# Retention/attention backbone, first projection stage: weights split at fixed points, a third PSUM bank for the second chunk, a shorter and earlier decay polynomial, transposes for the modulation pairs

## The chip, the cores and the metric

One Trainium2 chip, of which the kernel uses one core. The metric is the time of one execution on the device in microseconds (us). Kernels are compared by the median of several runs. The engines named below are PE (matrix multiply; PEld is its weight load), DVE (vector), ACT (scalar), POOL (GpSimd) and SP, whose queue issues nearly all DMAs.

## The reference, cut to what matters

The whole computation is two layers over 256 latent and 256 context tokens of width 2048: a bidirectional multi-scale retention layer, then a windowed attention layer. The change lies in the first stage, which makes the modulated input of layer 0 and the first head's queries and keys from it:

```python
mod = silu(c) @ ada_w[0] + ada_b[0]               # for c and for c_ctx
shift, scale, gate = split(mod, 3)
h = rms_norm(x, norm_gain[0]) * (1 + scale) + shift   # 512 tokens, width 2048
p = h @ ret_w_in                                    # q, k, v and gate of 8 heads
lg = log_sigmoid(decay_logit)                       # per head and direction
decay(i, j) = exp(lg * (i - j))                     # weights of the retention
```

All matrix products are wanted in nearly full float32. The kernel gets this by splitting each float32 operand into a high and a low part that TensorE can multiply, and by adding three products (high by high, low by high, high by low).

## The kernel before

Tokens lie on the free axis (512 columns, latents first), features on the partitions in 16 blocks `kb` of 128. Weights come in pieces of 128 x 2 x 512 (two feature blocks, 512 output columns). `load_w` (lines 120 to 130) loads a piece into `wraw`, copies its high part `wh` on ACT (L115) and subtracts for the low part `wl` on DVE (L112). `wraw`, `wh` and `wl` have three buffers each.

The first stage works through nine units of feature blocks, [0], [1], [2,3], [4,5], ... [14,15], and interleaves two jobs. For the next unit it makes the modulation; for the present one it multiplies.

- `strip(u)` (L363 to L375) loads the shift and scale columns of the adaLN matrix for the unit, four `araw` tiles of 1 MB (half that for the two single units), seven buffers in all, and multiplies them with silu(c) into one PSUM tile, 32 small matmuls in four column groups of the array.
- `strip_copy(u)` (L384) copies that PSUM tile to `ev` on ACT.
- `strip_turn(u)` (L386 to L409) turns `ev` so that features lie on the partitions and adds the four partial sums: one matmul of every 128-column block with a 2-column selection matrix (L393, eight rows in the trace for a pair). DVE then makes `gs` (L398), `sh` (L264) and the scaled input `ht` (L257); ACT makes the high part `hT_h` (L249) and DVE the low part `hl` (L250).
- `part0(kb)` (L423) multiplies one feature block with the weights of output chunk 0 (queries and keys of head 0). Its four accumulators `qk0` hold four PSUM banks through all nine units.
- `part1(kbs)` (L427 to L440) does the same for chunk 3, but with only one more bank of the five of that pool. For each of the four column groups j it accumulates over the unit alone and DVE adds the result to `qk1` in SBUF (L440). The groups take their banks in turn: j = 0 and 2 the fifth bank of the accumulator pool (`acc`), j = 1 and 3 a bank of a second pool (`pm`) of three, from which `strip` and `strip_turn` also take theirs.
- `decay_powers` (L286 to L318) makes log-sigmoid of the 16 decay logits with a polynomial, tiny DVE instructions that each wait for the one before, with two power operations on POOL. It is issued in unit 4 of the loop, behind that point's `wl`.

One iteration of the loop over u = 2 ... 8 is: `part0` of the unit's first block, `strip(u+1)`, `strip_copy`, the first four matmuls of `part0` of the second block, `strip_turn(u+1)`, the rest of `part0`, `part1`. After that the second stage (queries, keys, values and gates of all heads) begins, on PE without a pause.

What sets the order: each engine works its instructions in a fixed order, which a scheduler of the framework makes at build time from the program's order, the dependencies, free buffers and its own model of time. So an instruction that is ready early in that model can be placed ahead of others that come before it in the program. `tc.issue_after(x)` adds the rule that what is issued inside it comes behind instruction x on x's engine; `after()` (L357) uses it to keep PE in program order. `last_lo` holds the last `wl` of `load_w`.

## Time and profile before

| what | value |
|---|---|
| median of 3 runs (lowest, highest) | 2025.41 us (2024.19, 2025.95) |
| the profiled execution's own time | 2024.71 us |
| its span, first to last instruction | 2022.7 us |
| mean granted clock of TensorE | 0.997 |
| PE busy | 1985.5 us (98%) |
| DVE, ACT, POOL busy | 1163.5, 706.7, 239.6 us |
| first stage, from the span's start to the second stage's first matmul | 167.5 us |

Times in the profile count from the span's start. In a group row the two numbers behind the bar are the busy time and the mean duration of one instruction, then the idle time of the engine just before them and what ended it. In a timeline row the first number is the start, the second the duration, and the square brackets hold the idle time before it and its releaser. A matmul of 512 columns shows as 0.39 us because it is pipelined; what it costs in a row of them is the distance between starts, 0.23 us.

### The profile page before, as it was taken

Reading aid. Unit: us, or ns where it says so; the run is one execution under the profiler, and the core shown is the slowest. Engines: PE = TensorE matmul, PEld = TensorE weight load, DVE = VectorE, ACT = ScalarE, POOL = GpSimd, SP = SyncE. Lnnn points to the kernel's source line nnn. Section 1 sums busy time; section 2 is a strip of 40 time slices with the busy share of each in tenths; the row PEclk is TensorE's granted clock in tenths of the full one; section 3 lists DMA queues with packets and bytes.
Section 4 is the critical chain, followed back from the end, with each engine's and each line's share of the span. In section 5 each row is a group of like instructions: output and inputs, shape, how many; then the busy total and the mean of one; then the engine's idle time right before and its main releaser. Section 6 shows DMA issues by size and latency. Waiting matters only on the chain.

```text
span 2022.7 us, 24898 instructions
## 1 busy us (share of the span) xinstructions
PE 1985.5 (98%) x9376; PEld 1630.2 (81%) x9376; DVE 1163.5 (58%) x2316; ACT 706.7 (35%) x1074; POOL 239.6 (12%) x89
## 2 busy tenths in 40 slices
PE   5899999999999999999999999999999999999999
PEld 3568888888888888888888888888888888888887
DVE  4646323778678678687465344432332665777765
ACT  4224223323233232232232233422222444666653
POOL 0190401302203104004000000000000010000001
PEclk9999999999999999999999999999999999999999
DMA  9943224565555556555555324732332234444455
GB/s 373 399 186 103 88 87 146 175 203 170 175 192 175 180 176 194 177 176 179 187 187 167 116 93 156 267 128 94 104 113 95 94 99 146 146 135 136 146 190 175
DMA packets 116504, 330.11 MB, mean 163 GB/s; under 512 B 12192, under 2 KB 22560, under 8 KB 112160
## 3 DMA queue, kind: packets, MB, share of 16 engines
q1 hardware_dynamic: 107168, 315.95, 47.3%
q10 hardware_dynamic: 9216, 12.59, 1.7%
q8 instruction: 73, 1.20, 0.2%
q14 instruction: 47, 0.39, 0.1%
HBM read 315.90 MB, written 12.58 MB: 162 GB/s over the span
## 4 chain that ended last, share of the span: by engine, by line
PE 93%; DMA 2%; DVE 2%; issue 1%; ACT 1%; SPq 0%; POOL 0%; ACTq 0%; POOLq 0%; DVEq 0%
PE acc L135 24%; PE acc L137 24%; PE acc L136 24%; PE acc L176 6%; PE acc L178 3%; PE pm L135 3%; PE pm L136 3%; PE pm L137 2%; PE acc L423 2%; PE pm L375 1%; DMA wraw<-uT_d 1%; PE pm L944 1%; PE pm L660 1%; DMA araw<-in_adaS 1%; DMA wraw<-in_w 0%
## 5 line engine op out<-in xcount | busy, mean ns | idle before, releaser
L112 DVE TENSOR_TENSOR wl<-wraw,wh 128x1024 fp32r<-128x1024 f32 x368 | 451.5, 1227 | 631.4 <-ACT wh L115 630.8
L115 ACT CAST wh<-wraw 128x1024 fp32r<-128x1024 f32 x368 | 387.1, 1052 | 1002.1 <-PE acc L137 494.9
L137 PE MATMUL acc<-wh,hl 128*128 128x512 f32 x1216 | 473.9, 390 | 0.0
L135 PE MATMUL acc<-wh,hT_h 128*128 128x512 f32 x1088 | 426.6, 392 | 0.0
L136 PE MATMUL acc<-wl,hT_h 128*128 128x512 f32 x1088 | 423.8, 390 | 0.0
L539 DVE SCALAR_TENSOR_TENSOR ajunk<-abraw,crow 128x512 bf16<-128x512 f32 x448 | 308.4, 688 | 11.2 <-ACT crow L528 2.8
L135 PE MATMUL acc<-hT_h,wh 128*128 128x512 f32 x672 | 264.6, 394 | 9.1 <-DVE qk L440 9.1
L137 PEld LDWEIGHTS acc<-wh,hl 128*128 128x128 f32 x1216 | 228.2, 188 | 48.7 <-DVE hl L250 0.8
L136 PE MATMUL acc<-hl,wh 128*128 128x512 f32 x672 | 262.2, 390 | 0.0
L137 PE MATMUL acc<-hT_h,wl 128*128 128x512 f32 x672 | 261.1, 390 | 0.0
L135 PEld LDWEIGHTS acc<-wh,hT_h 128*128 128x128 f32 x1088 | 204.4, 188 | 41.4 <-issue 0.3
L136 PEld LDWEIGHTS acc<-wl,hT_h 128*128 128x128 f32 x1088 | 204.4, 188 | 41.0
L602 POOL TENSOR_TENSOR dd<-two,dd 128x128 f32<-128x128 f32 x8 | 167.3, 20922 | 537.7 <-DVE dd L600 537.7
L223 POOL TENSOR_TENSOR rs<-ms,mhalf 128x1 f32<-128x1 f32 (+2 forms) x47 | 41.7, 887 | 1026.8 <-DVE ms L217 691.1
L135 PEld LDWEIGHTS acc<-hT_h,wh 128*128 128x128 f32 x672 | 126.4, 188 | 40.9 <-DVE qk L440 11.8
L137 PEld LDWEIGHTS acc<-hT_h,wl 128*128 128x128 f32 x672 | 126.4, 188 | 26.5
L136 PEld LDWEIGHTS acc<-hl,wh 128*128 128x128 f32 x672 | 126.5, 188 | 25.4
L176 PE MATMUL acc<-hl,wh 128*128 128x512 f32 x256 | 92.2, 401 | 0.0
L176 PE MATMUL acc<-hT_h,wh 128*128 128x512 f32 x256 | 89.3, 394 | 0.0
L135 PE MATMUL acc<-wh,hl 128*128 128x512 f32 x192 | 75.5, 393 | 0.0
L136 PE MATMUL acc<-wl,hl 128*128 128x512 f32 x192 | 74.9, 390 | 0.0
L178 PE MATMUL acc<-hl,wl 128*128 128x256 f32 x256 | 72.0, 281 | 0.0
(230 smaller groups left out, 2405.5 us busy)
## 6 DMA issues: line engine op xcount, KB each, us to landing
wraw<-in_w SPq DMA_DIRECT2D x272, 512.0 KB, 3.5
abraw<-in_adaB SPq DMA_DIRECT2D x256, 256.0 KB, 3.2
wraw<-in_wo SPq DMA_DIRECT2D x96, 512.0 KB, 3.5
araw<-in_adaS SPq DMA_DIRECT2D x28, 1024.0 KB, 11.5
uT_d<-ue ACTq DMA_DIRECT2D x32, 256.0 KB, 2.1
wraw<-uT_d SPq DMA_DIRECT2D x16, 512.0 KB, 4.1
araw<-in_adaS SPq DMA_DIRECT2D x8, 512.0 KB, 9.5
x<-in_xT SPq DMA_DIRECT2D x4, 1024.0 KB, 7.5
```

The lines of the kernel that those rows point to most:

```text
L112: return nc.vector.tensor_tensor(out=out, in0=a, in1=hi.bitcast(F32), op=ALU.subtract)
L115: nc.scalar.copy(hi, src)
L135: nc.tensor.matmul(ps, lhsT=ah, rhs=bh, start=start, stop=False, skip_group_check=skip)
L136: nc.tensor.matmul(ps, lhsT=ah, rhs=bl, start=False, stop=False, skip_group_check=skip)
L137: return nc.tensor.matmul(ps, lhsT=al, rhs=bh, start=False, stop=stop, skip_group_check=skip).ins
L176: nc.tensor.matmul(accs[j], lhsT=wh[:, k2, js], rhs=h1(kb, s).rearrange("p a t -> p (a t)"), start=(kb == 0), stop=False)
L178: nc.tensor.matmul(accs[j][:, 0:L], lhsT=wl[:, k2, js], rhs=h1(kb, s)[:, 0], start=False, stop=(kb == 2 * nkp - 1))
L223: nc.gpsimd.tensor_tensor(out=rs, in0=ms, in1=mhalf.to_broadcast([P, n]), op=ALU.pow)
L375: last = nc.tensor.matmul(strips[u][32 * j:32 * j + 32, :n], lhsT=cpad[:, 4 * g + j, :], rhs=raw[:, j, :n], start=(g == 0), stop=(g == 3))
L423: last = nc.tensor.matmul(qk0[j], lhsT=a_[:, kb % 2, j * P:(j + 1) * P], rhs=b_, start=(kb == 0 and p == 0), stop=(kb == KB - 1 and p == 2))
L539: nc.vector.scalar_tensor_tensor(out=junk, in0=raw, scalar=1.0, in1=crow[:, t, q * 512:(q + 1) * 512], op0=ALU.mult, op1=ALU.mult, accum_o ...
L602: nc.gpsimd.tensor_tensor(out=dd, in0=two.to_broadcast([P, P]), in1=dd, op=ALU.pow)
```

## The change

Six edits, all in the first stage.

1. **Splits at fixed points.** Loading and splitting of a weight piece come apart (`load_raw`, `split_w`). In the loop, chunk 0's next piece is split at the start of an iteration and chunk 3's next piece at its end. `last_lo` and the new `last_hi` now also follow `part1`'s additions and the last `hT_h`, so these splits are queued behind them on DVE and ACT, and `strip_turn` is queued behind chunk 0's split.
2. **Order of loads on SP.** The four `araw` tiles of a unit are issued in one piece, then chunk 3's and chunk 0's next weights; before, chunk 0's weights came between the second and third tile. The constants `cst` come one unit earlier.
3. **Banks of `part1`.** j = 0 and 3 take the `acc` bank, j = 1 and 2 a `pm` bank each.
4. **Decay polynomial.** Addition and multiplication of a step go into one instruction (9 instead of 18, and two fewer around them). The first part with its POOL power (`decay_exp`) is placed at the kernel's start, the rest behind the second weight split, before the turn of unit 1.
5. **Transposes.** For pairs, `strip_turn` transposes the four blocks of `ev` and lets DVE add the four partial sums (`reduce_sum` into `tv`); single units keep the matmuls.
6. **Start.** All four groups of `strip(0)` go ahead of the four transposes in `token_rstd`; the first `wl` is made behind unit 0's modulation.

The diff, cut to what is spoken of:

```diff
--- before.py
+++ after.py
@@ -115,7 +115,7 @@
         nc.scalar.copy(hi, src)
         return sub(lo, src, hi)
 
-    last_lo = [None]
+    last_lo, last_hi = [None], [None]
 
     def load_raw(src):
         t = strm.tile([P, 2, 512], F32, name="wraw", tag="wraw", bufs=3)
@@ -123,10 +123,13 @@
         return t
 
     def load_w(src):
-        raw = load_raw(src)
+        return split_w(load_raw(src))
+
+    def split_w(raw):
         wh = strm.tile([P, 2, 512], F32R, name="wh", tag="wh", bufs=3)
         wl = strm.tile([P, 2, 512], F32R, name="wl", tag="wl", bufs=3)
-        last_lo[0] = split(wh, wl, raw).ins
+        last_hi[0] = nc.scalar.copy(wh, raw).ins
+        last_lo[0] = sub(wl, raw, wh).ins
         return wh, wl
 
     def mm3(ps, a, b, start, stop, skip=False):
@@ -236,9 +239,11 @@
         rs = rms_scale(pool, [sp[:, n * i:n * i + n] for i in range(len(parts))], n, 1.0 / D)
         bp = m_tile()
         if between is not None:
-            between()
-        for t in range(n):
-            nc.tensor.transpose(bp[:, (b0 + t) * P:(b0 + t + 1) * P], rs[:, t:t + 1].to_broadcast([P, P]), ident)
+            behind = between()
+        with tc.issue_after(behind) if between is not None else ExitStack():
+            for t in range(n):
+                nc.tensor.transpose(bp[:, (b0 + t) * P:(b0 + t + 1) * P], rs[:, t:t + 1].to_broadcast([P, P]),
+                                    ident)
         return bp
 
     def modulate(t, kb, sh, dst, kinds=(0, 1)):
@@ -246,9 +251,10 @@
         for s in kinds:
             c = slice(s * L, (s + 1) * L)
             hi, lo = dst(s)
-            nc.scalar.activation(hi, t[:, c], AF.Identity, bias=sh[:, kb, s:s + 1])
-            nc.vector.scalar_tensor_tensor(out=lo, in0=t[:, c], scalar=sh[:, kb, s:s + 1],
-                                           in1=hi.bitcast(F32), op0=ALU.add, op1=ALU.subtract)
+            last_hi[0] = nc.scalar.activation(hi, t[:, c], AF.Identity, bias=sh[:, kb, s:s + 1]).ins
+            last = nc.vector.scalar_tensor_tensor(out=lo, in0=t[:, c], scalar=sh[:, kb, s:s + 1],
+                                                  in1=hi.bitcast(F32), op0=ALU.add, op1=ALU.subtract)
+        return last.ins
 
     def scaled(t, src, kb, gs, rB, kinds=(0, 1)):
 
@@ -283,28 +289,31 @@
     def wide(tag, name, bufs=1):
         return pb.tile([P, 512], F32, name=name, tag=tag, bufs=bufs)
 
-    def decay_powers():
-
-        xl = vec[:, V_LGT:V_LGT + 16]
-
-        def sm(nm):
-            return pb.tile([P, 16], F32, name=nm, tag=nm)
-        ax, e, t, t2, acc = sm("ax"), sm("e"), sm("t"), sm("t2"), sm("lacc")
+
+    xl = vec[:, V_LGT:V_LGT + 16]
+
+    def sm(nm):
+        return pb.tile([P, 16], F32, name=nm, tag=nm)
+
+    def decay_exp():
+        ax, e = sm("ax"), sm("e")
         nc.vector.tensor_scalar(out=ax, in0=xl, scalar1=-1.0, scalar2=None, op0=ALU.mult)
         nc.vector.tensor_tensor(out=ax, in0=ax, in1=xl, op=ALU.max)
         nc.vector.tensor_scalar(out=ax, in0=ax, scalar1=-LOG2E, scalar2=None, op0=ALU.mult)
         nc.gpsimd.tensor_tensor(out=e, in0=two.to_broadcast([P, 16]), in1=ax, op=ALU.pow)
+        return e
+
+    def decay_powers(e):
+        t, t2, acc = sm("t"), sm("t2"), sm("lacc")
         nc.vector.tensor_scalar(out=t2, in0=e, scalar1=2.0, scalar2=None, op0=ALU.add)
         nc.vector.reciprocal(t2, t2)
         nc.vector.tensor_tensor(out=t, in0=e, in1=t2, op=ALU.mult)
         nc.vector.tensor_tensor(out=t2, in0=t, in1=t, op=ALU.mult)
-        nc.vector.memset(acc, 2.0 / 19)
+        nc.vector.tensor_scalar(out=acc, in0=t2, scalar1=2.0 / 19, scalar2=None, op0=ALU.mult)
         for k in range(8, -1, -1):
-            nc.vector.tensor_tensor(out=acc, in0=acc, in1=t2, op=ALU.mult)
-            nc.vector.tensor_scalar(out=acc, in0=acc, scalar1=2.0 / (2 * k + 1), scalar2=None, op0=ALU.add)
-        nc.vector.tensor_tensor(out=acc, in0=acc, in1=t, op=ALU.mult)
-        nc.vector.tensor_scalar(out=t, in0=xl, scalar1=0.0, scalar2=None, op0=ALU.min)
-        nc.vector.tensor_tensor(out=acc, in0=t, in1=acc, op=ALU.subtract)
+            nc.vector.scalar_tensor_tensor(out=acc, in0=acc, scalar=2.0 / (2 * k + 1), in1=t2 if k else t,
+                                           op0=ALU.add, op1=ALU.mult)
+        nc.vector.scalar_tensor_tensor(out=acc, in0=xl, scalar=0.0, in1=acc, op0=ALU.min, op1=ALU.subtract)
         nc.vector.tensor_scalar(out=lg2, in0=acc, scalar1=LOG2E, scalar2=None, op0=ALU.mult)
 
         expn = cst[:, C_EXPN:C_EXPN + 64].rearrange("p (a b) -> p a b", a=8)
@@ -333,6 +342,8 @@
         nc.vector.tensor_copy(cpad[:, :, 0:2], cact)
         ab1 = const.tile([P, KB], F32, name="ab1")
         nc.vector.tensor_scalar(out=ab1, in0=ab[:, 0, 1, :], scalar1=1.0, scalar2=None, op0=ALU.add)
+
+        e = decay_exp()
 
 
         for i in range(9):
@@ -385,15 +396,28 @@
 
         def strip_turn(u, rB):
 
+            with tc.issue_after(last_lo[0]), tc.issue_after(last_hi[0]):
+                return modulation(u, rB)
+
+        def modulation(u, rB):
             kbs, ev = units[u], evs.pop(u)
             nb = len(kbs)
             tp = m_tile()
             with after():
                 for b in range(2 * nb):
-                    last = nc.tensor.matmul(tp[:, 2 * b:2 * b + 2], lhsT=ev[:, b * P:(b + 1) * P],
-                                            rhs=vec[:, V_SEL:V_SEL + 2], start=True, stop=True)
+                    bs = slice(b * P, (b + 1) * P)
+                    if nb == 1:
+                        last = nc.tensor.matmul(tp[:, 2 * b:2 * b + 2], lhsT=ev[:, bs],
+                                                rhs=vec[:, V_SEL:V_SEL + 2], start=True, stop=True)
+                    else:
+                        last = nc.tensor.transpose(tp[:, bs], ev[:, bs], ident)
             pe[0] = last.ins
-            tv = tp[:, 0:4 * nb].rearrange("p (k n t) -> p k n t", n=2, t=2)
+            if nb == 1:
+                tv = tp[:, 0:4].rearrange("p (k n t) -> p k n t", n=2, t=2)
+            else:
+                tv = pb.tile([P, 2, 2, 2], F32, name="tv", tag="tv", bufs=2)
+                nc.vector.reduce_sum(tv.rearrange("p k n t -> p (k n) t"),
+                                     tp.rearrange("p (b g r) -> p b r g", b=4, g=4)[:, :, 0:2, :], axis=AX.X)
             for i, kb in enumerate(kbs):
                 nc.vector.scalar_tensor_tensor(out=gs0[:, kb, :], in0=tv[:, i, 1, :], scalar=ab1[:, kb:kb + 1],
                                                in1=ng[:, 0, kb:kb + 1].to_broadcast([P, 2]),
@@ -406,7 +430,9 @@
             if kbs[0] % 2 == 0:
                 hl[kbs[0] // 2] = r1.tile([P, 2, T], F32R, name="hl", tag=f"hl{kbs[0] // 2}")
             for kb in kbs:
-                modulate(ht[kb], kb, sh0, lambda s: (hT_h[:, kb, s * L:(s + 1) * L], h_l(kb)[:, s * L:(s + 1) * L]))
+                last = modulate(ht[kb], kb, sh0,
+                                lambda s: (hT_h[:, kb, s * L:(s + 1) * L], h_l(kb)[:, s * L:(s + 1) * L]))
+            return last
 
 
         qk0 = [acc_tile() for _ in range(4)]
@@ -427,7 +453,7 @@
         def part1(kbs, js_=range(4)):
             wh, wl = w[1]
             for j in js_:
-                ps = m_tile() if j % 2 else acc_tile()
+                ps = m_tile() if j in (1, 2) else acc_tile()
                 js = slice(j * P, (j + 1) * P)
                 with after():
                     for kb in kbs:
@@ -437,46 +463,59 @@
                 if kbs[0] == 0:
                     nc.scalar.copy(qk1[:, j, :], ps)
                 else:
-                    nc.vector.tensor_tensor(out=qk1[:, j, :], in0=ps, in1=qk1[:, j, :], op=ALU.add)
+                    last_lo[0] = nc.vector.tensor_tensor(out=qk1[:, j, :], in0=ps, in1=qk1[:, j, :],
+                                                         op=ALU.add).ins
 
         def first():
             strip(0, [0, 1])
-            w[0] = load_w(w0_d[0, 0])
+            w[0] = load_raw(w0_d[0, 0])
+            strip(0, [2, 3])
+            return pe[0]
 
         bp = token_rstd(pb, [ssq], between=first)
-        strip(0, [2, 3])
+        raw0 = w[0]
+        w[0] = [strm.tile([P, 2, 512], F32R, name=nm, tag=nm, bufs=3) for nm in ("wh", "wl")]
+        nc.scalar.copy(w[0][0], raw0)
         strip_copy(0)
-        strip_turn(0, bp)
+        last = modulation(0, bp)
+        with tc.issue_after(last):
+            last_lo[0] = sub(w[0][1], raw0, w[0][0]).ins
         rB = wide("aacc0", "rB")
         nc.scalar.copy(rB, bp)
         part0(0)
         strip(1, [0, 1])
         w[1] = load_w(w0_d[3, 0])
         strip(1, [2, 3])
+        nc.sync.dma_start(out=cst, in_=cst_d)
+        raw0 = load_raw(w0_d[0, 1])
+        with tc.issue_after(last_lo[0]):
+            decay_powers(e)
         strip_copy(1)
         part1([0], [0])
         strip_turn(1, rB)
         part1([0], [1, 2, 3])
         part0(1)
-        strip(2, [0, 1])
-        nc.sync.dma_start(out=cst, in_=cst_d)
-        w2 = load_w(w0_d[0, 1])
-        strip(2, [2, 3])
+        strip(2)
+        raw1 = load_raw(w0_d[3, 1])
+        w2 = split_w(raw0)
+        raw0 = load_raw(w0_d[0, 2])
         strip_copy(2)
         part1([1], [0])
         strip_turn(2, rB)
         part1([1], [1, 2, 3])
+        w1n = split_w(raw1)
         for u in range(2, 9):
             a_, b_ = units[u]
-            w[0], w[1] = w2, load_w(w0_d[3, u - 1])
+            w[0], w[1] = w2, w1n
+            if u < 8:
+                with tc.issue_after(last_lo[0]), tc.issue_after(last_hi[0]):
+                    w2 = split_w(raw0)
             part0(a_)
             if u < 8:
-                strip(u + 1, [0, 1])
-                w2 = load_w(w0_d[0, u])
-                if u == 4:
-                    with tc.issue_after(last_lo[0]):
-                        decay_powers()
-                strip(u + 1, [2, 3])
+                strip(u + 1)
+                raw1 = load_raw(w0_d[3, u])
+                if u < 7:
+                    raw0 = load_raw(w0_d[0, u + 1])
                 strip_copy(u + 1)
                 part0(b_, [0])
                 strip_turn(u + 1, rB)
@@ -484,6 +523,9 @@
             else:
                 part0(b_)
             part1([a_, b_])
+            if u < 8:
+                with tc.issue_after(last_lo[0]), tc.issue_after(last_hi[0]):
+                    w1n = split_w(raw1)
         if dbg:
             dbg("sh0", sh0), dbg("gs0", gs0)
             dbg("gam", gam)
```

## The prediction

> **What bounds the kernel now.** I read the page first, then the sums of waits, then the first stage in the chain of waits and, for one unit at a time, in the timelines of PE, DVE and ACT.
>
> ```profile
> span 2022.7 us, 24898 instructions
> PE 1985.5 (98%) x9376; PEld 1630.2 (81%) x9376; DVE 1163.5 (58%) x2316; ACT 706.7 (35%) x1074; POOL 239.6 (12%) x89
> DMA  9943224565555556555555324732332234444455
> GB/s 373 399 186 103 88 87 146 175 203 170 175 192 175 180 176 194 177 176 179 187 187 167 116 93 156 267 128 94 104 113 95 94 99 146 146 135 136 146 190 175
> ```
>
> PE is busy for 98% of the span. A microsecond that PE loses in the first stage is therefore a microsecond of the whole, as long as nothing later waits for a clock of its own; PE goes from the first stage into the second without idling, so I carry a gain there to the end one for one. The DMA rows say that the first two slices (to 101 us) are another regime: the DMA engines are full.
>
> Where PE waits inside the stage, to 170 us:
>
> ```profile
> PE acc L135 <- DVE qk L440: 9.1, 6, 4.1
> ```
>
> Six waits, one in each of the units 2 to 7, all for the addition that empties the bank of `part1`. One is 4.1 us, the others 1.0 us each. The other wait lies earlier, and the chain of waits shows it (start, duration, what), with PE's timeline below:
>
> ```profile
> 41.88 13.04 DMA araw<-in_adaS
> ```
> ```profile
> 51.73 2.78 PE L375 MATMUL pm<-araw,cpad 128*32 128x512 f32 x24
> 54.97 1.06 PE L375 MATMUL pm<-araw,cpad 128*32 128x512 f32 x8 [0.45 <-DMA araw<-in_adaS]
> 55.96 1.20 PE L423 MATMUL acc<-hT_h,wh 128*128 128x512 f32 x4
> ```
>
> The last tile of `strip(3)` lands at 41.88 + 13.04 = 54.92 us, and PE stands for it.
>
> ```profile
> 40.00:50.00 10.00, 9.67 (x61) 5.34 (x60) 5.37 (x14) 3.25 (x6) 0.00 (x0) 1.00 1.02 419
> araw<-in_adaS SPq DMA_DIRECT2D x28, 1024.0 KB, 11.5
> wraw<-in_w SPq DMA_DIRECT2D x20, 512.0 KB, 9.5
> ```
>
> At 419 GB/s and a DMA share of 1.02 the engines are saturated, and the landing is set by the bytes ahead of it. This is the hinge of the prediction. The change reorders the loads ahead of that tile but leaves the same bytes there: `cst` and chunk 0's and 3's weights for unit 2 and chunk 0's for unit 3 are ahead of it in both versions. So the 54.92 stays, `strip(3)` ends at 55.96 as now, and what the change wins before it (start, units 0 to 2, turn of unit 2) is lost in a longer wait there. All gains are counted from 55.96 on.
>
> After it a unit brings 4 x 1024 + 2 x 512 KB = 5.24 MB, 12.5 us at 419 GB/s. A unit on PE lasts 16.87 us now (the first two rows below) and 15.15 after the change: DMA no longer sets the pace there.
>
> **The regular wait (edits 1 and 3).** Unit 6, PE, then DVE, then ACT:
>
> ```profile
> 122.85 1.07 PE L423 MATMUL acc<-hT_h,wh 128*128 128x512 f32 x4
> 139.72 1.07 PE L423 MATMUL acc<-hT_h,wh 128*128 128x512 f32 x4
> ```
> ```profile
> 130.27 0.95 PE L393 MATMUL pm<-vec,ev 128*128 128x2 f32 x8
> 131.07 1.16 PE L423 MATMUL acc<-hl,wh 128*128 128x512 f32 x4
> 135.47 0.39 PE L137 MATMUL pm<-hT_h,wl 128*128 128x512 f32 x1
> 136.87 0.50 PE L135 MATMUL acc<-hT_h,wh 128*128 128x512 f32 x1 [1.01 <-DVE qk L440]
> 137.21 0.40 PE L136 MATMUL acc<-hl,wh 128*128 128x512 f32 x1
> ```
> ```profile
> 131.25 0.35 DVE L398 SCALAR_TENSOR_TENSOR gs<-pm,ab,vec 128x2 f32<-128x2 f32 x2 [6.07 <-PE pm L393]
> 133.40 1.22 DVE L112 TENSOR_TENSOR wl<-wraw,wh 128x1024 fp32r<-128x1024 f32 x1 [0.16 <-ACT wh L115]
> 134.55 1.67 DVE L250 SCALAR_TENSOR_TENSOR hl<-ht,sh,hT_h 128x256 fp32r<-128x256 f32 x4
> 136.13 0.68 DVE L440 TENSOR_TENSOR qk<-acc,qk 128x512 f32<-128x512 f32 x1
> ```
> ```profile
> 132.32 1.05 ACT L115 CAST wh<-wraw 128x1024 fp32r<-128x1024 f32 x1 [2.36 <-PE acc L423]
> ```
>
> Group j = 1 starts its last matmul at 135.47 and j = 2 can only start at 136.87, when DVE has added j = 0. Starts in a full row are 0.23 apart, so this costs 1.40 - 0.23 = 1.17, and the next start comes 0.34 instead of 0.23 later: 1.28 us for the unit. The addition is late because a weight split, ready early, went between `ht` and `hl`: `wh` at 132.32 and `wl` at 133.40 take about 1.15 us of DVE's time.
>
> After the change that split is queued behind the last addition. Then the first addition starts near 136.13 - 1.15 = 135.0. And j = 2 has a bank of its own: only j = 3 needs j = 0's, 18 matmuls after `part1` begins. That start is 12 matmuls before 135.47 + 0.23, at 132.98, and some 0.4 earlier after edit 5, so the bank is wanted at 132.54 + 18 x 0.227 = 136.62. An addition at 135.0 frees it at 135.0 + 0.74 = 135.74 (136.87 - 136.13 = 0.74). Each of the two edits would nearly do alone; together 0.9 us remain to spare. Five regular units (2, 3, 5, 6, 7): 5 x 1.28 = **6.4 us**.
>
> What the waits added by edit 1 hold up: behind chunk 3's split on DVE stand chunk 0's split and the next turn, but DVE idled 6.07 us before `gs`, and two splits take 2 x 1.22. Behind chunk 0's `wh` on ACT stands `hT_h`, more than 5 us later. `reduce_sum` (edit 5) adds one small DVE instruction, about 0.2 us as the other small ones here, before `gs`; it lies within the 0.9 and costs nothing.
>
> **Unit 4 (edit 4).** The polynomial now sits on DVE before unit 5's modulation:
>
> ```profile
> 95.95 0.39 PE L137 MATMUL pm<-hT_h,wl 128*128 128x512 f32 x1
> 100.47 0.80 PE L135 MATMUL acc<-hT_h,wh 128*128 128x512 f32 x1 [4.13 <-DVE qk L440]
> 105.75 1.27 PE L423 MATMUL acc<-hT_h,wh 128*128 128x512 f32 x4
> 106.86 1.08 PE L423 MATMUL acc<-hl,wh 128*128 128x512 f32 x4
> ```
>
> The wait is 4.52 - 0.23 = 4.29. Then the clock is at half: 12 matmuls take 105.75 - 100.47 = 5.28 instead of 2.72 (2.56 lost), four more 1.11 instead of 0.91 (0.20). Sum **7.05 us**. It goes whole, if the polynomial's new place costs nothing:
>
> ```profile
> L303 DVE TENSOR_TENSOR lacc<-lacc,t x9: 174/176/177, 90.1 to 93.4; 128x16 f32<-128x16 f32 x9
> 35.56 0.22 DVE L398 SCALAR_TENSOR_TENSOR gs<-pm,ab,vec 128x2 f32<-128x2 f32 x1 [4.94 <-PE pm L393]
> ```
>
> Sixteen steps took 3.3 us, 0.21 each. The 18 instructions left take 3.8 us, and DVE idles 4.94 us at that place. If that cover were gone, the delay still falls before the wait for DMA: PE reached `strip(3)` at 51.73 and, as 24 of its matmuls take 2.8 us, could come at 52.1 without loss, besides what edits 5 and 6 bring it earlier. On POOL the powers move into idle time.
>
> **Transposes (edit 5).** Eight matmuls of a turn run from 130.27 to 131.07, 0.80 us. Four transposes of the same shape stand later in the trace:
>
> ```profile
> 294.58 0.60 PE L660 MATMUL pm<-ident,sg 128*128 128x128 f32 x4
> 294.94 0.48 PE L135 MATMUL acc<-wh,hT_h 128*128 128x512 f32 x1
> ```
>
> 0.36 us, so 0.44 less for each of the six turns behind 55.96: **2.6 us**. Bounds: 0 (PE waits for `ev` instead) to 2.6; the row is of the very operation, so I take it.
>
> **What it may cost.** First, the clock. The longer wait at `strip(3)`, with PE early by an estimated 1 to 2 us (edit 5's 0.44 and edit 6), may cool it. The trace has such a place (PE busy is the second number; then granted clock, DMA share, GB/s):
>
> ```profile
> 24.00:26.00 2.00, 1.50 (x21) 0.78 (x20) 0.00 (x0) 0.37 (x1) 0.00 (x0) 1.00 1.06 381
> 26.00:28.00 2.00, 0.23 (x4) 0.15 (x3) 1.54 (x6) 0.96 (x3) 0.00 (x0) 0.91 1.09 352
> 28.00:30.00 2.00, 2.00 (x5) 1.61 (x6) 1.07 (x3) 1.36 (x2) 0.00 (x0) 0.50 1.11 410
> 30.00:32.00 2.00, 2.00 (x8) 1.61 (x7) 0.62 (x1) 0.00 (x0) 0.00 (x0) 0.74 1.01 418
> ```
>
> PE was busy 1.73 of 4 us, and the clock went to half for 0.36 + 2.00 + 1.04 = 3.4 us. That stretch does 8 instead of 15 matmuls, 7 x 0.227 = 1.6 us lost. At `strip(3)` two tiles of four would be awaited, 0.86 us of work every 2.5 us: as thin as that row, for about as long. Bounds 0 to 1.6; as it depends on how such stretches fall, I take a third, **0.5 us**. [...] The trace's fall came with waits under 2 us, so I keep the term.
>
> Second, the end of the stage:
>
> ```profile
> 167.51 0.39 PE L135 MATMUL acc<-wh,hT_h 128*128 128x512 f32 x1
> ```
> ```profile
> 165.55 0.41 DVE L571 TENSOR_TENSOR t<-acc,ropeR 128x256 f32<-128x256 f32 x1
> 167.71 0.69 DVE L440 TENSOR_TENSOR qk<-pm,qk 128x512 f32<-128x512 f32 x1
> ```
>
> The last addition (j = 3) ends at 168.40, 0.9 us after the second stage begins. After the change j = 3 sits in an `acc` bank. If the second stage's first product is given that bank, PE waits 0.9; `qk0`'s first bank is free from 165.96, and I take 0.
>
> **Sum.** 6.4 + 7.05 + 2.6 - 0.5 = 15.6 us. From the profiled execution's 2024.71 this gives 2009.1; the median lies 0.7 above that execution, hence 2009.8.
>
> **Rivals.**
>
> *The queue of loads (slower).* On SP, chunk 0's next weights now stand ahead of all four `araw` tiles, and they need the `wraw` buffer that chunk 3's split frees, about 2 us into a unit.
>
> ```profile
> wraw<-in_w SPq DMA_DIRECT2D x272, 512.0 KB, 3.5
> ```
>
> With an empty queue the weights land 3.5 us later, the tiles 2.5 us apart behind them, the last at 2 + 3.5 + 10 = 15.5 of that unit. It is wanted in the next one, at 15.15 + 2.7 (the first block's `part0`, 12 x 0.227) + 2.8 = 20.7. So 5 us are to spare, and this decides once the split runs over 5 us later: placed behind the next turn instead, at about 13, the tile lands at 26.5 and PE waits 5.8 in each of five units, 29 us: 2039. For it speaks that the split is now bound to later instructions; against it that these end at the unit's start. 4%.
>
> *DVE stays late.* If two splits still came before the first addition, it would start near 137.4 and free the bank at 138.1, 1.5 after it is wanted: five units, 7.5 us, 2017.3. The written order speaks against it. 6%.
>
> *Transposes gain nothing*, since `ev` on ACT ends just before them: 2012.4. 8%.
>
> *The clock falls at `strip(3)` every time*, or the bank at the end is the wrong one: 1 us more, 2010.9. 16%.
>
> *The tile lands earlier* or early gains come through: up to 1.5 us less, 2008.3. 8%.
>
> *The change does not act*: the waits remain, 2025. 1%.
>
> **How the numbers follow.** The forecast has 57%. The range 2007 to 2014 holds it and the three rivals nearest to it (89%), less their edges. About 0.2% (4 us) can be told from no change. Faster by more: all but the slower case, the one without effect and a little for what I have not seen: 0.94; the same 0.02; slower 0.04.
>
> **What would show it.** Right: `strip(3)` still ends at about 56 us; units of 15.1 to 15.2 us after it; no wait of PE for L440's addition; the second stage's first matmul near 152; a turn of 0.36 us. Wrong: PE waiting for `araw` in units 4 to 7 (the queue), for additions (DVE), a half clock after 56 us, or a changed second stage.

## The result, and the profile after

| | before | after |
|---|---|---|
| median of 4 runs each, us (lowest, highest) | 2025.68 (2024.19, 2027.09) | 2010.47 (2010.32, 2012.41) |
| profiled execution's own time, us | 2024.71 | 2010.32 |
| span, us | 2022.7 | 2008.5 |
| `strip(3)` ends (start of the first `part0` matmul behind it), us | 55.96 | 56.02 |
| second stage starts, us | 167.51 | 151.42 |

The ratio of the times is 0.9927 (95% interval 0.991 to 0.9944): 15.2 us off the median, where 15.6 had been predicted.

Two names help below. The end of a strip is the start of the first matmul behind its 32; the expectations call the end of `strip(3)` the start of unit 3, although by the program the second block of unit 2 begins there. A round runs from the end of one strip to the end of the next; the round behind `strip(5)` holds the turn of unit 5 and the `part1` of unit 4.

The page of after, the same four rows as were shown of before:

```profile
span 2008.5 us, 24836 instructions
PE 1980.4 (99%) x9348; PEld 1626.7 (81%) x9348; DVE 1162.3 (58%) x2312; ACT 706.5 (35%) x1074; POOL 238.8 (12%) x89
DMA  9872234556555555555554324833232234444455
GB/s 378 360 267 84 95 102 152 186 178 192 176 174 183 186 181 175 190 179 166 202 173 163 116 95 151 284 110 105 96 111 98 95 100 155 139 138 134 149 188 168
```

PE is busy for only 5 us less, though the span is 14.2 shorter: what went is mostly waiting, the rest matmuls at half clock (before's granted clock was 0.50 from 101 to 105 us) and the 28 that the transposes spare. The third slice now carries 267 GB/s instead of 186: the rounds follow each other faster and ask for the same bytes in less time.

The sum of PE's waits to 155 us no longer has L440's addition (L466 now). Behind `strip(3)` no wait is left; up to its end these two are the longest, PE's very first one aside (the wait, then us in total, times, longest us):

```profile
PE acc L449 <- ACT hT_h L254: 1.8, 1, 1.8
PE pm L386 <- DMA araw<-in_adaS: 1.3, 1, 1.3
```

PE's timeline of after: `strip(3)` (L386), the new turn with transposes (L413), and the round behind `strip(5)` as an example:

```profile
50.97 2.78 PE L386 MATMUL pm<-araw,cpad 128*32 128x512 f32 x24
55.03 1.07 PE L386 MATMUL pm<-araw,cpad 128*32 128x512 f32 x8 [1.27 <-DMA araw<-in_adaS]
56.02 1.19 PE L449 MATMUL acc<-hT_h,wh 128*128 128x512 f32 x4
57.06 0.60 PE L413 MATMUL pm<-ident,ev 128*128 128x128 f32 x4
57.41 1.17 PE L449 MATMUL acc<-hl,wh 128*128 128x512 f32 x4
...
86.32 1.20 PE L449 MATMUL acc<-hT_h,wh 128*128 128x512 f32 x4
...
92.36 0.39 PE L138 MATMUL pm<-hT_h,wh 128*128 128x512 f32 x1
...
93.72 0.39 PE L138 MATMUL acc<-hT_h,wh 128*128 128x512 f32 x1
...
101.46 1.20 PE L449 MATMUL acc<-hT_h,wh 128*128 128x512 f32 x4
```

and the step at which the first stage ends, with the load that `strip(3)` stood for, from the chain of waits:

```profile
151.42 0.39 PE L138 MATMUL acc<-wh,hT_h 128*128 128x512 f32 x1
```
```profile
41.18 13.80 DMA araw<-in_adaS
```

Read them in this order. PE came to `strip(3)` at 50.97 instead of 51.73 and stood there for 1.27 instead of 0.45 us, because the last tile landed at 41.18 + 13.80 = 54.98, as before (54.92). So `strip(3)` ends where it did, 0.06 later. From there on a round takes about 101.46 - 86.32 = 15.14 us instead of 16.87. This one, with unit 4's `part1`, had taken 112.36 - 89.72 = 22.64 before (the two rows below, of the kernel before), and now takes as long as the others. The turn is 57.41 - 57.06 = 0.35 us instead of 0.80. The second stage starts 16.09 us earlier.

```profile
89.72 1.19 PE L423 MATMUL acc<-hT_h,wh 128*128 128x512 f32 x4
...
112.36 1.19 PE L423 MATMUL acc<-hT_h,wh 128*128 128x512 f32 x4
```

DVE of after in the same round:

```profile
87.99 0.19 DVE L419 TENSOR_REDUCE tv<-pm 128x8 f32<-128x32 f32 x1 [4.90 <-PE pm L413]
90.33 1.67 DVE L255 SCALAR_TENSOR_TENSOR hl<-ht,sh,hT_h 128x256 fp32r<-128x256 f32 x4
91.92 0.68 DVE L466 TENSOR_TENSOR qk<-acc,qk 128x512 f32<-128x512 f32 x1
95.88 2.35 DVE L112 TENSOR_TENSOR wl<-wraw,wh 128x1024 fp32r<-128x1024 f32 x2
```

Both weight splits (`wl`) stand behind the last addition, none is between `ht` and `hl`. The first addition ends at 92.60; the bank that it empties is wanted at 93.72, by j = 3, and `j = 2` started on a `pm` bank at 92.36 without asking for it. The margin is 1.1 us; 0.9 had been predicted.

### The profile page after: what moved, and what is told of

It reads as the page before. It is cut to its first block, busy times and chain, and to the rows that moved or that the text cites. A ratio compares the mean times of both kernels' runs of the same rounds, so it can differ in the third digit from the quotient of the medians.

```text
span 2008.5 us, 24836 instructions
## 1 busy us (share of the span) xinstructions
PE 1980.4 (99%) x9348; PEld 1626.7 (81%) x9348; DVE 1162.3 (58%) x2312; ACT 706.5 (35%) x1074; POOL 238.8 (12%) x89
## 4 chain that ended last, share of the span: by engine, by line
PE 96%; DMA 2%; DVE 1%; issue 0%; ACT 0%; SPq 0%; POOL 0%; POOLq 0%; ACTq 0%; DVEq 0%
PE acc L138 24%; PE acc L139 24%; PE acc L140 24%; PE acc L179 6%; PE acc L181 3%; PE pm L138 3%; PE pm L139 3%; PE pm L140 3%; PE acc L449 2%; PE pm L386 1%; DMA wraw<-uT_d 1%; PE pm L986 1%; PE pm L702 1%; DMA araw<-in_adaS 1%; DMA xp<-in_xT 0%
```

## The experiments

The theory is the prediction's: behind the end of `strip(3)` PE lost time to three things, the late addition, the polynomial and the long turn, and the change removes each by the edit named for it; ahead of it one tile sets the time. Its rivals: that the banks or the splits do the work alone; that the polynomial's length counts and not its place; that the tile isn't what fixes the end of `strip(3)`. Edit 6 and the earlier load of the constants were not undone by themselves. Each kernel below is the changed kernel with one thing undone or moved, and computes the same. For each, the stretch from the end of `strip(3)` to the second stage is the cleanest measure: it contains no wait for DMA, and two profiles of the changed kernel agree in it to 0.01 us. Starts are PE's, in us, from each kernel's profile; times and ratios are against the kernel before on the same chip.

| kernel | `strip(3)` ends | second stage starts | between | median, us | ratio (95%) |
|---|---|---|---|---|---|
| before | 55.96 | 167.51 | 111.55 | 2025.68 | |
| after | 56.02 | 151.42 | 95.40 | 2010.47 | 0.9927 (0.991 to 0.9944) |
| bank_old | 55.75 | 153.78 | 98.03 | 2012.76 | 0.9933 (0.9916 to 0.9949) |
| splits_old | 56.43 | 151.97 | 95.54 | 2010.7 | 0.9923 (0.9908 to 0.9938) |
| both_old | 56.33 | 160.02 | 103.69 | 2018.43 | 0.9961 (0.9946 to 0.9976) |
| turn_old | 56.00 | 154.08 | 98.08 | 2013.8 | 0.9936 (0.9921 to 0.9951) |
| decay_late | 56.51 | 157.62 | 101.11 | 2016.4 | 0.9949 (0.9935 to 0.9964) |
| decay_short_late | 56.15 | 151.59 | 95.44 | 2010.93 | 0.9922 (0.9906 to 0.9939) |
| decay_long_early | 55.95 | 151.39 | 95.44 | 2010.69 | 0.9921 (0.9907 to 0.9936) |
| w_behind | 55.59 | 151.02 | 95.43 | 2010.24 | 0.9919 (0.9904 to 0.9934) |
| after_2 (one run) | 56.28 | 151.69 | 95.41 | 2009.32 | |
| w_behind_2 (one run) | 55.55 | 150.96 | 95.41 | 2008.63 | |

### The banks and the splits, alone and together

`bank_old` gives `part1` its old banks and keeps the new places of the splits:

```diff
-                ps = m_tile() if j in (1, 2) else acc_tile()
+                ps = m_tile() if j % 2 else acc_tile()
```

> The changed kernel with the banks of part1 as before (j = 0 and 2 in acc, j = 1 and 3 in pm); the fixed points of the splits stay. Theory 1 (either edit alone does nearly all): the addition of j = 0 comes about 1.15 us earlier than before, so j = 2 waits 0 to 0.2 us per unit; the second stage starts at 151.4 to 152.5 us instead of 151.4, the whole 2010.5 to 2011.5. Theory 2 (the bank is what removes the wait): 1.28 us in each of the units 2 to 7, second stage at about 159, whole 2018.

`splits_old` keeps the new banks and takes the old splits and, in the loop, the old order of loads (edit 1 undone, and edit 2 but for the earlier constants):

```diff
-            w[0], w[1] = w2, w1n
-            if u < 8:
-                with tc.issue_after(last_lo[0]), tc.issue_after(last_hi[0]):
-                    w2 = split_w(raw0)
+            w[0], w[1] = w2, load_w(w0_d[3, u - 1])
             part0(a_)
             if u < 8:
-                strip(u + 1)
-                raw1 = load_raw(w0_d[3, u])
-                if u < 7:
-                    raw0 = load_raw(w0_d[0, u + 1])
+                strip(u + 1, [0, 1])
+                w2 = load_w(w0_d[0, u])
+                strip(u + 1, [2, 3])
...
             part1([a_, b_])
-            if u < 8:
-                with tc.issue_after(last_lo[0]), tc.issue_after(last_hi[0]):
-                    w1n = split_w(raw1)
```

> The changed kernel with the splits and the order of loads as before, with part1's new banks. Theory 1: a split stands between ht and hl again and the addition of j = 0 starts about 1.1 us later, but only j = 3 wants its bank, so PE waits 0 to 0.3 us per unit; second stage at 151.4 to 153, whole 2010.5 to 2012. Theory 2 (the order is what removes the wait): 1.28 us per unit, second stage at about 159, whole 2018.

`both_old` undoes all of these.

> The changed kernel with both the banks and the splits as before; decay, transposes and start stay as changed. Theory 1: the regular wait is back whole in units 2 to 7 (unit 4 now as any other), 6 x 1.28 = 7.7 us: second stage at 159.1, whole 2018.2. Rival (the wait had another cause, as the later turn or the polynomial): second stage below 154.

Measured, between the end of `strip(3)` and the second stage: 8.29 us more with both undone, 2.63 with the old banks alone, 0.14 with the old splits alone. The `part1` of six units lies there (2 to 7), so these make 1.38, 0.44 and 0.02 a unit. For bank_old, theory 1 is missed by its own range (0 to 0.2 a unit) and theory 2 by far. First both_old, a round on DVE and the same place on PE:

```profile
93.20 1.22 DVE L112 TENSOR_TENSOR wl<-wraw,wh 128x1024 fp32r<-128x1024 f32 x1
94.34 1.67 DVE L255 SCALAR_TENSOR_TENSOR hl<-ht,sh,hT_h 128x256 fp32r<-128x256 f32 x4
95.92 0.69 DVE L465 TENSOR_TENSOR qk<-acc,qk 128x512 f32<-128x512 f32 x1
```
```profile
89.38 1.20 PE L448 MATMUL acc<-hT_h,wh 128*128 128x512 f32 x4
...
96.66 0.50 PE L138 MATMUL acc<-hT_h,wh 128*128 128x512 f32 x1 [1.09 <-DVE qk L465]
```

This is the old picture: a split lies between `ht` and `hl`, the addition starts 95.92 - 89.38 = 6.54 us into the round, and j = 2 waits for it. Then bank_old:

```profile
90.94 1.67 DVE L255 SCALAR_TENSOR_TENSOR hl<-ht,sh,hT_h 128x256 fp32r<-128x256 f32 x4
92.53 0.68 DVE L466 TENSOR_TENSOR qk<-acc,qk 128x512 f32<-128x512 f32 x1
```
```profile
86.93 1.20 PE L449 MATMUL acc<-hT_h,wh 128*128 128x512 f32 x4
...
92.76 0.39 PE L140 MATMUL pm<-hT_h,wl 128*128 128x512 f32 x1
93.27 0.50 PE L138 MATMUL acc<-hT_h,wh 128*128 128x512 f32 x1
```

The split is gone from its place and the addition starts 92.53 - 86.93 = 5.60 us into the round, 0.94 earlier. j = 2 still comes 93.27 - 92.76 = 0.51 after the matmul ahead of it, 0.28 more than in a full row, and the few starts behind it are stretched as well; this makes the 0.44. The sum of PE's waits does not name it; it shows in the distance between starts. In splits_old the addition is late again, but asked for later:

```profile
93.28 0.69 DVE L465 TENSOR_TENSOR qk<-acc,qk 128x512 f32<-128x512 f32 x1
```
```profile
92.80 0.39 PE L138 MATMUL pm<-hT_h,wh 128*128 128x512 f32 x1
...
94.16 0.40 PE L138 MATMUL acc<-hT_h,wh 128*128 128x512 f32 x1
```

j = 2 begins on its own bank at 92.80, before the addition has begun; the addition ends at 93.97, 0.2 us before j = 3 starts. So the bank does by itself what both do together, with a margin of 0.2 instead of 1.1 us, and the splits do two thirds of it.

### The turn

`turn_old` lets the pairs use the selection matmuls again:

```diff
-                    if nb == 1:
+                    if True:
                         last = nc.tensor.matmul(tp[:, 2 * b:2 * b + 2], lhsT=ev[:, bs],
...
-            if nb == 1:
-                tv = tp[:, 0:4].rearrange("p (k n t) -> p k n t", n=2, t=2)
+            if True:
+                tv = tp[:, 0:4 * nb].rearrange("p (k n t) -> p k n t", n=2, t=2)
```

> The changed kernel with the selection matmuls in place of the transposes for pairs. Theory 1: 0.44 to 0.46 us more in each of six turns behind 56 us, nothing ahead of it: strip(3) still ends at 56.0, second stage at 154.1, whole 2013.1. Rival (the turns ahead of the DMA wait count too): 3.1 us and strip(3) later. Rival (the turn hides behind another wait): 0.

```profile
88.24 0.95 PE L410 MATMUL pm<-vec,ev 128*128 128x2 f32 x8
89.05 1.17 PE L449 MATMUL acc<-hl,wh 128*128 128x512 f32 x4
```

A turn takes 0.81 instead of 0.35 us, and the stage 2.68 us more: six turns of 0.45. The extra DVE instruction of the new turn (0.19 us) costs nothing.

### The decay polynomial: length or place

`decay_late` takes the old polynomial (18 instructions for the nine steps) and puts it with its exponential back into unit 4, behind the split of chunk 0's next weights:

```diff
-        e = decay_exp()
...
-        with tc.issue_after(last_lo[0]):
-            decay_powers(e)
...
                     w2 = split_w(raw0)
+            if u == 4:
+                with tc.issue_after(last_lo[0]):
+                    decay_powers(decay_exp())
```

> The changed kernel with the whole long polynomial, exponential included, back in unit 4 behind that point's weight split. DVE starts it some 3.4 us into the unit and ends it at about 12.8 (0.6 + 2.9 POOL + 5.6), where the turn wants DVE at 7.9; part1's first addition comes at about 17 instead of 12.5, and j = 3 wants the bank at 14. Theory 1: PE waits about 3 us in that unit, with the third bank taking 1.3 us off the old 4.3; if the clock falls too, up to 2.7 us more. Second stage at 154.5 to 157.5, whole 2013.5 to 2016.5. Rival (the place does not matter, only the new order of the splits did): 151.4.

`decay_short_late` has the short polynomial in that late place and leaves the exponential at the start, so that its call reads:

```diff
+            if u == 4:
+                with tc.issue_after(last_lo[0]):
+                    decay_powers(e)
```

> The changed kernel with the short polynomial in unit 4 (the exponential stays at the start). 18 instructions, 3.8 us, start about 3.4 us into the unit and end at 7.2, before the turn wants DVE at 7.9. Theory 1: no wait of PE, second stage at 151.4 to 151.7, whole 2010.5: the place is not needed once the polynomial is short and the power gone. Rival (the early place is what pays): some of the 4.3 us returns, second stage over 153.

`decay_long_early` has the old polynomial in the new, early place:

```diff
-            nc.vector.scalar_tensor_tensor(out=acc, in0=acc, scalar=2.0 / (2 * k + 1), in1=t2 if k else t,
-                                           op0=ALU.add, op1=ALU.mult)
+            nc.vector.tensor_tensor(out=acc, in0=acc, in1=t2, op=ALU.mult)
+            nc.vector.tensor_scalar(out=acc, in0=acc, scalar1=2.0 / (2 * k + 1), scalar2=None, op0=ALU.add)
```

> The changed kernel with the long polynomial (28 instructions in place of 18) at the early place. It takes 2.1 us more on DVE ahead of unit 1's turn and delays that turn by about 1 us. Theory 1 (the DMA wait at strip(3) takes it up): strip(3) starts about 1 us later, waits about 1 us less and ends at 56.0 all the same; second stage at 151.4, whole 2010.5. Rival (early delays reach the end): second stage at 152.4 to 153.5.

decay_late is 5.71 us longer; the other two lie within 0.04 us of the changed kernel. In decay_late, DVE stands for POOL's exponential first, then works through the polynomial, and the turn's `reduce_sum` comes behind it:

```profile
87.12 0.17 DVE L308 TENSOR_SCALAR t<-e 128x16 f32<-128x16 f32 x1 [3.01 <-POOL e L303]
...
93.32 0.18 DVE L420 TENSOR_REDUCE tv<-pm 128x8 f32<-128x32 f32 x1
...
97.44 0.68 DVE L467 TENSOR_TENSOR qk<-acc,qk 128x512 f32<-128x512 f32 x1
```
```profile
98.18 0.50 PE L138 MATMUL acc<-hT_h,wh 128*128 128x512 f32 x1 [3.78 <-DVE qk L467]
```

The round began at 86.83, so `reduce_sum` comes 6.49 us into it; in the changed kernel 87.99 - 86.32 = 1.67. Of these 4.8 us the margin of 1.1 swallows its part and the rest is PE's wait of 3.78 for j = 3's bank, which is followed by half a clock (granted clock is the third number from the end):

```profile
99.00:101.00 2.00, 2.00 (x7) 1.53 (x6) 0.98 (x3) 1.04 (x1) 2.00 (x1) 0.54 0.00 0
101.00:103.00 2.00, 2.00 (x7) 1.61 (x6) 2.00 (x3) 0.01 (x1) 2.00 (x1) 0.61 0.00 0
```

In decay_short_late the chain runs in the same place, but begins without POOL and is done before the turn, with 0.28 us to spare:

```profile
86.36 0.17 DVE L317 TENSOR_SCALAR lg<-lacc 128x16 f32<-128x16 f32 x1
...
88.12 0.19 DVE L419 TENSOR_REDUCE tv<-pm 128x8 f32<-128x32 f32 x1 [0.28 <-PE pm L413]
```

So either place does for the short chain, and either length does in the early place. The early place alone is enough; in the late place, the short chain with its exponential done beforehand is enough. How much of the latter is the shorter chain and how much the exponential was not tried apart; the 3.01 us of waiting for POOL are the larger part of the 4.8.

### The tile that fixes the end of `strip(3)`

`w_behind` moves chunk 0's weights for unit 3, half a megabyte, behind all tiles of `strip(3)`, and splits them inside unit 2's `part1`:

```diff
         w2 = split_w(raw0)
-        raw0 = load_raw(w0_d[0, 2])
         strip_copy(2)
...
                 strip(u + 1)
+                if u == 2:
+                    raw2 = load_raw(w0_d[0, 2])
...
-            part1([a_, b_])
+            part1([a_, b_], [0])
+            if u == 2:
+                with tc.issue_after(last_lo[0]), tc.issue_after(last_hi[0]):
+                    w2 = split_w(raw2)
+            part1([a_, b_], [1, 2, 3])
```

> The changed kernel with one load moved: chunk 0's weights for unit 3 are loaded behind the four tiles of strip(3) instead of ahead of them, and split between part1's first and second group of unit 2. 0.5 MB less ahead of the tile that PE waits for. Theory 1 (the landing of that tile is set by the bytes ahead of it): it lands 1.25 us earlier, at 53.7, PE's wait of 1.27 us there goes to about 0, strip(3) ends at 54.7, second stage at 150.1 to 150.3, whole 2009.2. Rival (the landing is set by when the tile is issued, at 41.2 us, when its buffer comes free): it lands at 55 as before, whole 2010.5. A second rival: the late split stalls the start of unit 3 by up to 1 us and eats the gain.

```profile
51.97 3.69 PE L386 MATMUL pm<-araw,cpad 128*32 128x512 f32 x32
55.59 1.21 PE L449 MATMUL acc<-hT_h,wh 128*128 128x512 f32 x4
```

PE goes through all 32 matmuls without standing, and `strip(3)` ends at 55.59, 0.43 earlier. The missing wait has two causes. PE came to `strip(3)` at 51.97, a whole microsecond later than in the changed kernel's profile; and the tile landed at 54.55, 0.43 earlier, just as PE came to the eight matmuls that need it. In decay_short_late, where PE came as late as here (51.80), the tile landed at 55.11. So neither expectation is met: the tile moved, but by 0.43 to 0.56 of the 1.25 us that half a megabyte takes at 419 GB/s (before's rate from 40 to 50 us). What the DMA queues had moved, from the span's start to the landing, in the changed kernel and in w_behind:

```profile
DMA packets 7916, 20.86 MB, mean 379 GB/s; under 512 B 529, under 2 KB 4753, under 8 KB 6889
```
```profile
DMA packets 7777, 20.34 MB, mean 373 GB/s; under 512 B 517, under 2 KB 4741, under 8 KB 6751
```

So 0.52 MB less went ahead of the tile. Over the ten profiles that keep the bytes this sum lies between 20.50 and 21.04 MB, and it is 20.41 in w_behind's second profile, so a part of the difference may be scatter. But already at 20 us, before the two kernels' loads differ, this execution had moved 6.49 MB and the changed kernel's 6.80; those 0.31 MB are 0.74 us at 419 GB/s, which would be most of what the landing failed to gain. Why this execution was behind so early isn't known. The whole time doesn't tell the two kernels apart: 2010.24 (2009.28 to 2010.99) against 2010.47.

### Two second profiles

In the changed kernel's profile the second stage starts 16.1 us earlier, but the span is only 14.2 shorter. To see where the difference arises, the changed kernel and `w_behind` were each profiled once more.

> The changed kernel, profiled a second time. From the second stage's first product to PE's last product the kernel before took 1850.2 us and the changed one 1851.9; the difference builds up in the last 60 us, where 32 x 128-column pairs of products start every 0.347 us in the one and every 0.353 us on average (0.361, 0.349 and 0.350 in turn) in the other. Theory: the pace there is fixed by the kernel's own order of work, so this run again takes 1851.5 to 1852.5 us for that stretch and ends near 2008.5. Rival: the pace is one of several into which any execution can fall, whatever the kernel; then this run may take 1850 to 1851 for the stretch and end near 2007. Both expect unit 3 to start within 0.5 us of 56.0, units of 15.1 to 15.2 us and the second stage at 151.4 plus or minus 0.5.

> The version in which chunk 0's weights for unit 3 are loaded behind strip(3)'s tiles, profiled a second time. In its first profile PE never stood for strip(3), so the start of unit 3 hangs on when PE began: 10.94 us after unit 1's start (44.65 to 55.59), where the changed kernel took 12.39 (43.63 to 56.02). Theory: as long as PE begins no more than 1 us earlier, unit 3 again starts 10.9 to 11.4 us after unit 1, and the stage's other units stay at 15.1 to 15.2. Rival: the load that was moved only happened not to count in that run; then unit 3 again starts near 56.0. On the end's pace: if it is the kernel's own, 1850.5 to 1851.2 us from the second stage's first product to PE's last one; if it is the execution's, it may be 1851.9 to 1852.4.

From the second stage's first matmul to PE's last one the kernel before took 1850.24 us, the changed kernel 1851.92 in its first profile and 1850.54 in its second; w_behind 1850.92 and 1850.66. Most of the loss, 1.3 us, lies in the last 70 us, a long row of matmuls of 512 and 256 columns in turn. A window of it, first profile and second profile of the changed kernel:

```profile
1960.00:1980.00 20.00, 20.00 (x115) 17.34 (x114) 9.67 (x9) 8.45 (x10) 2.12 (x2) 1.00 0.71 223
```
```profile
1960.00:1980.00 20.00, 20.00 (x117) 17.51 (x116) 10.08 (x10) 8.92 (x11) 1.92 (x2) 1.00 0.64 216
```

At the same granted clock, with PE busy throughout, 115 or 117 matmuls fit into 20 us; before had 118. Of the twelve profiles, six took 1850.2 to 1850.9 us from the second stage's first matmul to the last one, and six 1851.9 to 1852.4. The same kernel shows both, so the pace belongs to the execution and not to the change: that theory of a pace fixed by the order of work falls.

For `w_behind`, `strip(3)` ends 55.55 - 44.33 = 11.22 us behind `strip(2)` (the expectation's unit 1), where the changed kernel took 12.39 and 12.31. The moved load counts again: the tile lands at 54.51, against 54.98 and 55.24 in the changed kernel's two profiles. It is still what PE gets last, by a little, as the chain of waits of this second profile shows:

```profile
41.76 12.75 DMA araw<-in_adaS
...
54.56 1.06 PE pm L386 x8
```

## Why the prediction was right, point by point

**The hinge.** Landing 54.92 foretold, 54.98 measured; PE's wait grew from 0.45 to 1.27 and swallowed what came ahead of it. Over the changed kernel's two profiles and the seven variants that keep the bytes ahead of that tile, `strip(3)` ends between 55.75 and 56.51, though the end of `strip(2)` varies from 43.5 to 45.2. That the tile sets this is shown by the traces themselves: in eleven of the twelve profiles, w_behind's two among them, `strip(3)` ends 1.04 us after the tile landed, wherever between 54.51 and 55.47 that was. The one exception is decay_long_early, where PE came so late (52.38) that the tile was already there, and `strip(3)` ends 1.16 behind it. That the bytes ahead of the tile set the landing is supported by w_behind, though less than the 1.25 us came of it. As two profiles of one kernel lie 0.26 apart here, the agreement within 0.06 is partly luck. The old order of the loads makes little of it: 56.43 in splits_old.

**The regular wait: 6 x 1.28 foretold (one of them within unit 4's 7.05), 6 x 1.38 by both_old.** In one point the step was loose. "Each of the two edits would nearly do alone" holds for the bank (0.02 us left a unit), but the splits alone leave 0.44. The prediction's own numbers hold the reason: with the old banks, j = 2 wants the bank at 135.70, and 0.4 earlier with edit 5, while it is freed at 135.74. Besides, the addition came only 0.94 earlier instead of 1.15: with the split out of the way, `hl` waits a little for ACT's `hT_h` (0.10 us behind the end of `ht` in bank_old, 90.94 against 89.17 + 1.67).

**Unit 4: 7.05.** The round with unit 4's `part1` went from 22.64 to 15.14 us; less 0.45 for its turn that is 7.05. Of this edit 4 is worth 5.71 by itself (decay_late); the rest, 1.34, is the regular wait, which edits 1 and 3 remove. That the new place is free is shown by decay_long_early, where even the longer chain cost nothing there: PE came to `strip(3)` at 52.38, 1.41 later than in the changed kernel, and yet `strip(3)` ended at 55.95, because the wait of 1.27 was gone and the tile landed 0.19 earlier (54.79). Nothing was left to take up more, as PE and not the tile came last there.

**Transposes: 0.44 a turn and 2.6 in all foretold, 0.45 and 2.68 measured** (turn_old).

**The clock at `strip(3)`: 0.5 foretold, 0 measured.** This is the term that was mis-sized. It rested on the words that "two tiles of four would be awaited". Only the fourth was; PE had 24 matmuls to do while the third landed. The windows of after, the early fall and `strip(3)`:

```profile
26.00:28.00 2.00, 0.83 (x4) 0.70 (x5) 1.82 (x5) 1.79 (x4) 0.00 (x0) 1.00 1.11 351
28.00:30.00 2.00, 2.00 (x7) 1.58 (x6) 1.99 (x3) 0.54 (x1) 0.00 (x0) 0.63 1.08 405
52.00:54.00 2.00, 1.75 (x20) 0.26 (x8) 1.11 (x1) 0.00 (x0) 2.00 (x1) 1.00 1.00 393
54.00:56.00 2.00, 0.97 (x8) 0.16 (x8) 0.00 (x0) 0.00 (x0) 2.00 (x1) 1.00 1.03 393
```

At `strip(3)` PE was busy for 2.72 of 4 us and the clock stayed at 1.00, in this profile and in the eleven others; the four matmuls behind it take 57.06 - 56.02 = 1.04 us (1.03 to 1.05 in all twelve), where four at half clock took 31.46 - 29.62 = 1.84 us in the changed kernel (granted 0.63 and 0.52 in the two windows from 28 us on). The fall behind 28 us came where PE had been busy for 0.83 of the 2 us ahead and had waited for 1.77 at most. Why the clock fell there and not at `strip(3)`, where PE had waited for 1.27, is not shown.

**End of the stage: 0 foretold, 0 measured.** The second stage's first matmul (151.42) has no wait. From the end of `strip(3)` the sum without the clock is 16.05; measured are 111.55 - 95.40 = 16.15. Undone one at a time the parts come to 8.29 + 5.71 + 2.68 = 16.68: the regular wait is 0.1 a unit longer beside the short turn (1.38, both_old) than beside the long one (1.28, before), and six units have it.

**One for one to the end.** This held to 0.1 us until 1500 us behind the second stage's start. From there on the first profile lost 1.7 us, mostly to its pace of matmuls in the last 70 us, which no step of the prediction had, so that its span is 14.2 shorter than before's; in the second profile it is 15.4. Foretold were 15.6, with 0.5 taken off for a clock that did not fall: two small errors of opposite sign. That the forecast of 2009.8 lies only 0.7 from the median is therefore partly luck. The rival that lies nearest to the median, a clock that falls every time (2010.9), did not happen.

**The other rivals.** Behind the end of `strip(3)` there is no wait for `araw`: the last tile of each of the next five strips landed 2.8 to 5.0 us before PE wanted it, where 5 had been worked out. DVE was not late, and the transposes gained in full.

## What to carry to other kernels

When an accumulator's bank is what PE waits for, look first for another bank that is idle at that moment: here one `pm` bank did by itself what moving the splits did only to two thirds. Edits that remove the same wait do not add up: undone one by one, banks and splits cost 2.63 and 0.14 us, together 8.29. And find the first point whose time is fixed by something else, here the landing of one tile at 55 us, and count gains only behind it.

## What the runs showed of the hardware

- One row of matmuls, at full clock and without any wait, runs at more than one pace: 115 or 117 in 20 us in two executions of one kernel (1.4 us over the whole). What decides it isn't known; a difference of one to two microseconds between two single profiles can come from it.
- How long the clock stayed at half differed between stalls of nearly the same length. After before's wait of 4.13 us in unit 4 it was at half for 6.8 us (granted 0.58, 0.50, 0.50 and 0.72 in the four windows of 2 us from 99 us on), after decay_late's 3.78 for 3.4 (0.54 and 0.61, above). So the two cost 3.4 us more or less of half clock here. The two cases differ in when the clock fell: in before at about 99.3, 1.2 us ahead of PE's return at 100.47, and in decay_late at about 99.2, 1.0 us behind PE's return at 98.18 (both times from the granted clock of the window from 99 us on, 0.58 and 0.54). That this decides the length is not shown.
- The granted clock's column can be silent. In decay_long_early it reads 1.00 from 28 to 32 us, but the matmuls come at half pace there, four in 1.91 us, as in the changed kernel's profile, whose column shows the fall (four in 1.91 us from 29.62 us on, granted 0.63 and 0.52 in the same two windows):

```profile
28.00:30.00 2.00, 2.00 (x5) 1.59 (x6) 2.00 (x3) 1.14 (x2) 0.00 (x0) 1.00 1.09 389
```
```profile
29.65 1.91 PE L451 MATMUL acc<-hl,wh 128*128 128x512 f32 x4
```
